# Token tiles of an output projection in the order 0, 3, 1, 2, 4, 5, with the norm of a tile at a higher scheduling priority

## The chip, the core and the metric

The kernel runs on one core of one Trainium2 chip. The metric is the device time of one execution in microseconds (us). The engines are TensorE (PE in the profile; PEld is its weight load), VectorE (DVE), ScalarE (ACT), GpSimd (POOL) and SyncE (SP), which only issues DMAs here. Each engine runs its own instructions strictly in order and waits on semaphores for the others.

## The reference

The kernel computes an encoder trunk of two layers for 768 tokens (256 and 512) with 1024 features. Each layer has a token mixer and then a gated feed-forward part, and both stand between two norms:

```python
def rms_norm(x, g):
    y = x * lax.rsqrt(jnp.mean(x * x, axis=-1, keepdims=True) + RMS_EPS)
    return y * g

def swiglu(h, w_gate_up, w_down):
    g, u = jnp.split(h @ w_gate_up, 2, axis=-1)
    return (jax.nn.silu(g) * u) @ w_down

for i in range(DEPTH):
    h = rms_norm(x, norm_mix_pre[i])
    m = window_gqa_sink(h, ...) if i % 2 == 0 else diff_attention(h, ...)   # both end in  o @ w_o
    x = x + rms_norm(m, norm_mix_post[i])
    h = rms_norm(x, norm_ffn_pre[i])
    x = x + rms_norm(swiglu(h, ffn_w_gate_up[i], ffn_w_down[i]), norm_ffn_post[i])
```

## The kernel before, in words

The 768 tokens are six tiles of 128 (`t` = 0 to 5). Every large product is made of three matmuls on split operands: a value is cut into a rounded part (`hi`, a cast on ACT) and the remainder (`lo`, a subtraction on DVE), and hi x hi, lo x hi and hi x lo are summed in PSUM (lines 266 to 268). `two_parts` does that for weights (lines 201 and 202), `split` for activations (lines 254 and 255). Weights come by DMA into two raw buffers (`wraw`), are split into a ring of five slots (`whi`, `wlo`), and a raw buffer's next DMA may go as soon as the split has read it.

`project` multiplies the mixer's output by `w_o` in two halves of 512 columns. The second half and everything behind it is `staged`: for each token tile it runs 24 matmuls (`po`), the square sum on ACT (line 506), and the four stages that `finish` returns. `stage_a` takes the row's reciprocal root (`rstd`: ACT line 310, POOL line 311), `stage_b` adds the normed product to the residual `x` (DVE line 421), stores `x` by SP and starts the next norm (`row_rstd`: ACT lines 316 and 310, POOL line 311), `stage_c` scales `x` into `y_po` (DVE line 320), and `stage_d` transposes that tile on PE and stores it as the feed-forward's input. The stages of a tile are written one and two rounds behind its matmuls.

The feed-forward's gate and up products use a seven-product scheme on 2 x 2 blocks. Tokens are halved into tiles 0 to 2 and 3 to 5, features into two blocks of 512, and `stage_d` is then `combine`. For tiles 0 to 2 it copies and splits the transposed tile (a11, a12). For tile t from 3 on it also needs tile t - 3 and makes the sums s1 to s4 (DVE lines 400, 401, 402 and 406) and splits them: five ACT casts and a copy, nine DVE operations. The same combination on the weights' side is lines 223 to 226, and `b` is the split of one weight block. The products follow in `ffn`: `p1` and `p2` (`px`, tiles 0 to 2, two groups of 12 matmuls for each of the first four chunks), then for each chunk `p4` (`pz`, needs the split of tile 5's second half), `p6` (`py`, needs s2), `p5` (`pw`, needs s1), `p7` (`py`, needs s3) and `p3` (`pw`, needs s4). The `px` groups need tiles 0 to 2 alone. All others need all of tiles 3 to 5 combined.

Code is written in program order, but a scheduler sets the order on each engine by priority and by its own estimate of when inputs are ready. Priority is the place in the program, unless a block is put under `tc.high_priority()`. The order that results is fixed when the program is built.

Of the kernel before, what the change touches and what calls it, by code (L numbers as in the profile page):

```python
# [13 lines left out]
ALU = mybir.AluOpType  # L14
# [15 lines left out]
NT = 6  # L30
# [14 lines left out]
def trunk(  # L45
# [19 lines left out]
    nc = tc.nc  # L65
# [22 lines left out]
    for name, step, mult in (("mask_l", 1, -1), ("mask_r", -1, 1)):  # L88
        m = const.tile([P, P], BF16, name=name)
        nc.gpsimd.memset(m, 0.0)  # L90
        nc.gpsimd.affine_select(
            out=m, in_=m, compare_op=ALU.is_ge, fill=MASK, base=0,
# [213 lines left out]
    def rstd(ss, eps, name):  # L306

        w = ss.shape[1]
        r = small.tile([P, 8], F32, tag="rstd", name=f"rstd_{name}")
        state["rstd"] = nc.scalar.activation(out=r[:, :w], in_=ss, func=AF.Identity, bias=eps)  # L310
        nc.gpsimd.tensor_tensor(out=r[:, :w], in0=r[:, :w], in1=mhalf[:, :w], op=ALU.pow)
        return r[:, :w]

    def row_rstd(src, junk, name):
        ss = small.tile([P, 1], F32, tag="ss", name=f"ss_{name}")
        nc.scalar.activation(out=junk, in_=src, func=AF.Square, scale=D ** -0.5, accum_out=ss)
        return rstd(ss, eps_sb[:, 0:1], name)

    def scaled(y, src, r, g):
        state["scaled"] = nc.vector.scalar_tensor_tensor(out=y, in0=src, scalar=r, in1=g, op0=ALU.mult, op1=ALU.mult)  # L320
# [24 lines left out]
    def load_x(sub, t):  # L345
        x = xpool.tile([P, D], F32, tag="x", name=f"x{sub}_{t}")
        nc.sync.dma_start(out=x, in_=x_at[sub][t])
        return x

    def transposes(src, t, name, scale=None):  # L350

        half, at = t // 3, (t % 3) * P

        def step(b):
            tp = bank(f"tp_{name}_{b}")
            for j in range(4):
                k = 4 * b + j
                nc.tensor.transpose(tp[:, j * P:(j + 1) * P], src[:, k * P:(k + 1) * P], ident)
            v = tp.rearrange("p (k n) -> p k n", k=4)
            h4 = h_hi[half][:, 4 * b:4 * b + 4, at:at + P]  # L360
            l4 = h_lo[half][:, 4 * b:4 * b + 4, at:at + P]
            if scale is None:
                split(h4, l4, v)
            else:
                nc.scalar.activation(out=h4, in_=v, func=AF.Copy, scale=scale)
                nc.vector.scalar_tensor_tensor(
                    out=l4, in0=v, scalar=scale, in1=h4.bitcast(F32), op0=ALU.mult, op1=ALU.subtract)

        return [lambda: step(0), lambda: step(1)]

    def combine(src, t, name, comb, o):

        at = (t % 3) * P

        def turn(b):  # L380
            tp = bank(f"tp_{name}_{b}")
            for j in range(4):
                k = 4 * b + j
                nc.tensor.transpose(tp[:, j * P:(j + 1) * P], src[:, k * P:(k + 1) * P], ident)
            return tp

        v4 = lambda v: v.rearrange("p (k n) -> p k n", k=4)
        into = lambda half, b: tuple(v[half][:, 4 * b:4 * b + 4, at:at + P] for v in (h_hi, h_lo))
        if t < 3:
            for b in range(2):  # L390
                tp = turn(b)
                split(*into(0, b), v4(tp))
                nc.scalar.copy(out=o[t][:, b * 512:(b + 1) * 512], in_=tp)
            return
        a11, a12 = o[t - 3][:, :512], o[t - 3][:, 512:]
        s1, a22, s3, s2 = o[t][:, :512], o[t][:, 512:], src[:, :512], src[:, 512:]
        tp1, tp0 = turn(1), turn(0)
        nc.scalar.copy(out=a22, in_=tp1)
        split(*into(1, 1), v4(tp1))
        nc.vector.tensor_tensor(out=s1, in0=tp0, in1=a22, op=ALU.add)  # L400
        nc.vector.tensor_tensor(out=s3, in0=tp0, in1=a11, op=ALU.subtract)
        nc.vector.tensor_tensor(out=s2, in0=s1, in1=a11, op=ALU.subtract)
        split(*(v[:, :, at:at + P] for v in comb["s2"]), v4(s2))
        split(*into(1, 0), v4(s3))
        split(*(v[:, :, at:at + P] for v in comb["s1"]), v4(s1))
        nc.vector.tensor_tensor(out=a12, in0=a12, in1=s2, op=ALU.subtract)
        split(*(v[:, :, at:at + P] for v in comb["s4"]), v4(a12))

    def finish(sub, t, o, ssy, x, g, comb):

        r = {}
        m, (ss, y) = o[t], ssy

        def stage_a():
            r[0] = rstd(ss[:, 1:2], ss[:, 0:1], f"post{sub}_{t}")

        def stage_b():  # L420
            nc.vector.scalar_tensor_tensor(out=x, in0=m, scalar=r[0], in1=x, op0=ALU.mult, op1=ALU.add)
            nc.sync.dma_start(out=x_at[sub + 1][t], in_=x)
            if g is not None:
                r[1] = row_rstd(x, y, f"pre{sub + 1}_{t}")

        def stage_c():
            scaled(y, x, r[1], g)

        def stage_d():
            if comb is not None:  # L430
                combine(y, t, f"h{sub + 1}_{t}", comb, o)
                return
            for s in transposes(y, t, f"h{sub + 1}_{t}"):
                s()

        return [stage_a, stage_b] + ([stage_c, stage_d] if g is not None else [])

    def last_tile(sub, t, m, ssy, x, r):

        halves = [slice(0, 512), slice(512, 1024)]  # L440
        for c, q in zip(halves, (nc.sync, nc.scalar)):
            nc.vector.scalar_tensor_tensor(
                out=x[:, c], in0=m[:, c], scalar=r, in1=x[:, c], op0=ALU.mult, op1=ALU.add)
            q.dma_start(out=x_at[sub + 1][t][:, c], in_=x[:, c])

    def staged(sub, units, o, sq, g, comb=None):

        st = {}
        for t in range(NT):
            x = load_x(sub, t)
            units[t][0]()
            if t >= 2 and g is not None:
                st[t - 2][2]()
            if t >= 1:
                st[t - 1][1]()
            units[t][1]()
            if t >= 2 and g is not None:  # L460
                st[t - 2][3]()
            if g is None and t == NT - 1:
                last_tile(sub, t, o[t], sq[t], x, sq["last"])
                break
            st[t] = finish(sub, t, o, sq[t], x, g, comb)
            st[t][0]()
        if g is None:
            return []
        return [st[NT - 2][2], st[NT - 1][1], st[NT - 2][3], st[NT - 1][2], st[NT - 1][3]]
# [214 lines left out]
    def project(o, layer, sub, turn_o, gp, g_next, wk, sq, done):  # L684
        gs = ExitStack()
        gpool2 = gs.enter_context(tc.tile_pool(name=f"comb{layer}", bufs=1, side="right", reuse_waits="tile"))
        comb = {
            n: tuple(gpool2.tile([P, 4, HALF], F32R, name=f"{n}{part}_{layer}") for part in ("hi", "lo"))
            for n in ("s1", "s2", "s4")}
        for t in range(done, NT):  # L690
            if turn_o is not None and t + 1 < NT:
                for s in turn_o(t + 1):
                    s()
            for s in out_unit(t, wk, o, 0, gp, sq, f"po{layer}_0_{t}"):
                s()
        wk = column_blocks(take(4), 512)
        units = {}
        for t in range(NT):
            steps = []

            def half(i, t=t, steps=steps):
                if i == 0:
                    steps += out_unit(t, wk, o, 1, gp, sq, f"po{layer}_1_{t}")
                n = len(steps) // 2
                for s in (steps[:n] if i == 0 else steps[n:]):
                    s()

            units[t] = [lambda half=half: half(0), lambda half=half: half(1)]
        return staged(sub, units, o, sq, g_next, comb), comb, gpool2, gs
# [177 lines left out]
    def ffn(layer, later, comb, cpool, cstack, ostack, gains):  # L887
# [116 lines left out]
        with ExitStack() as st:  # L1004
# [17 lines left out]
            for n2 in range(2):  # L1022
# [21 lines left out]
                else:  # L1044
# [25 lines left out]
                    if final:  # L1070
# [3 lines left out]

                        tails[NT - 1] = [last_first, lambda: piece(1)]
                    rest = staged(sub, tails, y, sq, g_next)
        return rest

# [81 lines left out]
    def rows(name):  # L1160
        stack = ExitStack()
        pool = stack.enter_context(tc.tile_pool(name=name, bufs=1, reuse_waits="tile"))
        return [pool.tile([P, D], F32, name=f"{name}{t}") for t in range(NT)], stack
# [5 lines left out]
    o, ostack = rows("oa")  # L1169
    later, *held = mixer_a(*gains(0), ready, o)  # L1170
    later = ffn(0, later, *held, ostack, lambda: gains(1))
    o, ostack = rows("ob")
# [69 lines left out]
```

## Time and profile before

| | us |
|---|---|
| median of 3 runs | 1755.25 |
| lowest and highest of them | 1753.36, 1756.82 |
| the profiled execution, its own time | 1756.35 |
| its span in the profile | 1754.6 |
| PE busy in the span | 1712.0 |
| DVE, ACT and POOL busy | 1174.0, 856.0, 81.6 |

PE is the engine to look at: it is busy in all but 43 us of the span. The kernel is long and most of it is a row of stages in which PE waits for nothing, so the stretches where it does wait must be looked for. "PEclk" or granted clock tells the share of full speed that TensorE had: 1.00 is 2.4 GHz and 0.50 is 1.2 GHz. A matmul that runs at 1.2 GHz counts as busy too, so time lost to the clock is not in PE's idle time.

Times "at 300" are microseconds from the start of the span. Layer 0's stretch around the change is at 265 to 345, layer 1's at 1190 to 1270.

### The profile page before, as it was taken

The page shows a single profiled execution, that of the slowest core. Times are in us where ns is not written, and L with a number is a line of the kernel's source. Part 1 is how long each engine was busy: PE and PEld are TensorE (multiplying, and loading weights), DVE is VectorE, ACT ScalarE, POOL GpSimd, SP SyncE. Part 2 cuts the span into 40 slices and gives each one's busy share as a digit, 9 for nine tenths or more (in the row PEclk, how much of TensorE's full clock was granted, in tenths as well). Part 3 has the DMA queues.
Part 4 walks back from the last instruction along what each step waited for, and adds up shares of the span by engine and source line. Part 5 has one row for each costly group of instructions (what it writes and reads, how often), then busy time and mean ns, then how long its engine had stood idle before and what let it go on. Part 6 is the DMA issues. An engine that isn't in the chain of part 4 may idle for free.

```text
span 1754.6 us, 25701 instructions
## 1 busy us (share of the span) xinstructions
PE 1712.0 (98%) x9714; PEld 1559.3 (89%) x9714; DVE 1174.0 (67%) x2368; ACT 856.0 (49%) x1971; POOL 81.6 (5%) x126
## 2 busy tenths in 40 slices
PE   8999999899999999999999999999799999999997
PEld 7888878799999988888999999878799999988886
DVE  7788767887777744446767677756887777744433
ACT  6777766433333333435566666756433333334432
POOL 1000001000000000002000000501000000000000
PEclk9999999899999999999999999999899999999999
DMA  6111105333332266454211111115333322266454
GB/s 205 37 37 46 47 15 191 121 131 100 100 101 72 94 202 190 150 163 173 85 37 37 37 42 42 48 37 182 119 132 100 100 100 75 87 201 195 142 156 138
DMA packets 55485, 187.14 MB, mean 107 GB/s; under 512 B 6721, under 2 KB 7105, under 8 KB 55361
## 3 DMA queue, kind: packets, MB, share of 16 engines
q1 hardware_dynamic: 51696, 167.93, 30.0%
q0 software_dynamic: 3520, 17.30, 2.5%
q8 instruction: 76, 1.25, 0.3%
q14 instruction: 49, 0.39, 0.1%
q10 hardware_dynamic: 144, 0.26, 0.0%
HBM read 155.59 MB, written 29.88 MB: 106 GB/s over the span
## 4 chain that ended last, share of the span: by engine, by line
PE 86%; DVE 6%; issue 3%; DMA 2%; ACT 2%; POOL 1%; SPq 0%; DVEq 0%; POOLq 0%; ACTq 0%
PE pd L266 6%; PE pd L268 6%; PE pd L267 6%; PE pqb L266 4%; PE pqb L268 4%; PE py L266 4%; PE pqb L267 4%; PE py L267 3%; PE py L268 3%; PE pw L266 3%; PE pw L267 3%; PE pw L268 3%; PE px L268 3%; PE px L267 3%; PE px L266 3%
## 5 line engine op out<-in xcount | busy, mean ns | idle before, releaser
L202 DVE TENSOR_TENSOR wlo<-wraw,whi 128x1024 fp32r<-128x1024 f32 (+1 forms) x206 | 239.3, 1166 | 122.1 <-ACT whi L201 120.8
L201 ACT CAST whi<-wraw 128x1024 fp32r<-128x1024 f32 (+1 forms) x206 | 204.9, 1001 | 169.6 <-PE px L267 84.2
L266 PE MATMUL pd<-whi,ahi 128*128 128x512 f32 (+1 forms) x550 | 210.4, 383 | 3.8 <-ACT ahi L254 3.8
L267 PE MATMUL pd<-wlo,ahi 128*128 128x512 f32 (+1 forms) x550 | 210.1, 382 | 0.0
L268 PE MATMUL pd<-whi,alo 128*128 128x512 f32 (+1 forms) x550 | 209.6, 382 | 0.0
L255 DVE TENSOR_TENSOR alo<-araw,ahi 128x768 fp32r<-128x768 f32 x88 | 84.1, 958 | 156.3 <-ACT ahi L254 154.7
L254 ACT CAST ahi<-araw 128x768 fp32r<-128x768 f32 x88 | 73.5, 835 | 171.3 <-PE pd L267 101.4
L266 PE MATMUL pqb<-whi,hhi 128*128 128x384 f32 x384 | 136.5, 356 | 0.0
L268 PE MATMUL pqb<-whi,hlo 128*128 128x384 f32 x384 | 128.8, 335 | 0.0
L267 PE MATMUL pqb<-wlo,hhi 128*128 128x384 f32 x384 | 128.8, 335 | 0.0
L266 PEld LDWEIGHTS pd<-whi,ahi 128*128 128x128 f32 x550 | 103.7, 189 | 24.6 <-ACT ahi L254 4.7
L268 PEld LDWEIGHTS pd<-whi,alo 128*128 128x128 f32 x550 | 103.9, 189 | 20.2
L267 PEld LDWEIGHTS pd<-wlo,ahi 128*128 128x128 f32 x550 | 103.7, 189 | 19.6
L266 PE MATMUL px<-hhi,whi 128*128 128x384 f32 x352 | 118.3, 336 | 2.2 <-ACT sv L912 2.2
L268 PE MATMUL px<-hhi,wlo 128*128 128x384 f32 x352 | 117.6, 334 | 0.0
L267 PE MATMUL px<-hlo,whi 128*128 128x384 f32 x352 | 117.6, 334 | 0.0
L942 ACT ACTIVATE u<-u 128x384 f32<-128x384 f32 x44 | 23.1, 525 | 161.2 <-DVE u L941 161.2
L266 PE MATMUL po<-whi,hhi 128*128 128x512 f32 x192 | 77.9, 406 | 0.2 <-ACT hhi L254 0.2
L268 PE MATMUL po<-whi,hlo 128*128 128x512 f32 x192 | 75.5, 393 | 0.2 <-DVE hlo L255 0.2
L267 PE MATMUL po<-wlo,hhi 128*128 128x512 f32 x192 | 75.3, 392 | 0.0
L266 PE MATMUL pqa<-whi,hhi 128*128 128x384 f32 x192 | 74.1, 386 | 0.1
L266 PEld LDWEIGHTS pqb<-whi,hhi 128*128 128x128 f32 x384 | 72.3, 188 | 1.9 <-issue 1.7
(244 smaller groups left out, 4422.8 us busy)
## 6 DMA issues: line engine op xcount, KB each, us to landing
araw<-act SPq DMA_DIRECT2D x88, 384.0 KB, 3.3
wraw<-in_wgu SPq DMA_DIRECT2D x62, 512.0 KB, 3.5
wraw<-in_wd SPq DMA_DIRECT2D x44, 512.0 KB, 4.2
y_wraw<-in_wgu SPq DMA_DIRECT2D x34, 512.0 KB, 3.5
act<-st POOLq DMA_DIRECT2D x44, 384.0 KB, 2.6
wraw<-in_wb SPq DMA_DIRECT2D x32, 384.0 KB, 3.1
xd<-x SPq DMA_DIRECT2D x18, 512.0 KB, 3.0
x<-xd SPq DMA_DIRECT2D x18, 512.0 KB, 4.2
```

The costliest lines, as they stand in the source:

```text
L201: state["raw_hi"] = nc.scalar.copy(out=hi, in_=src)
L202: state["raw_lo"] = nc.vector.tensor_tensor(out=lo, in0=src, in1=hi.bitcast(F32), op=ALU.subtract)
L254: state["hi"] = nc.scalar.copy(out=hi, in_=src)
L255: state["lo"] = nc.vector.tensor_tensor(out=lo, in0=src, in1=hi.bitcast(F32), op=ALU.subtract)
L266: nc.tensor.matmul(out, ah, bh, start=start and i == 0, stop=False, skip_group_check=more)
L267: nc.tensor.matmul(out, ah, bl, start=False, stop=False, skip_group_check=more)
L268: nc.tensor.matmul(out, al, bh, start=False, stop=stop and i == last, skip_group_check=more)
L942: nc.scalar.activation(out=u, in_=u, func=AF.Silu)
```

## The change

The second half of the output projection takes the tiles in the order 0, 3, 1, 2, 4, 5 in place of 0 to 5, so that tile 3 can be combined as soon as tile 0 has been. The norm's steps in `finish` (the reciprocal roots, the residual sum, the square sum and the scaling) get a higher priority. They apply to all four passes through `staged`; the new order only to the two that combine (`comb is not None`).

```diff
         def stage_a():
-            r[0] = rstd(ss[:, 1:2], ss[:, 0:1], f"post{sub}_{t}")
+            with tc.high_priority():
+                r[0] = rstd(ss[:, 1:2], ss[:, 0:1], f"post{sub}_{t}")
         def stage_b():
-            nc.vector.scalar_tensor_tensor(out=x, in0=m, scalar=r[0], in1=x, op0=ALU.mult, op1=ALU.add)
+            with tc.high_priority():
+                nc.vector.scalar_tensor_tensor(out=x, in0=m, scalar=r[0], in1=x, op0=ALU.mult, op1=ALU.add)
+                if g is not None:
+                    r[1] = row_rstd(x, y, f"pre{sub + 1}_{t}")
             nc.sync.dma_start(out=x_at[sub + 1][t], in_=x)
-            if g is not None:
-                r[1] = row_rstd(x, y, f"pre{sub + 1}_{t}")
         def stage_c():
-            scaled(y, x, r[1], g)
+            with tc.high_priority():
+                scaled(y, x, r[1], g)
...
-        st = {}
-        for t in range(NT):
+        st = []
+        for i, t in enumerate((0, 3, 1, 2, 4, 5) if comb is not None else range(NT)):
...
-            st[t] = finish(sub, t, o, sq[t], x, g, comb)
-            st[t][0]()
+            st.append(finish(sub, t, o, sq[t], x, g, comb))
+            st[i][0]()
```

The indices of `st` in the loop become `i - 2` and `i - 1` in place of `t - 2` and `t - 1`. No instruction is added or removed, and lines below the edit shift by 2 to 5.

The program that is built shows where instructions go. In the rows below, names end in a serial number, and the digit before it is the tile or the chunk (`y_po_1_5` is tile 5, `px_0` chunk 0). The first place is DVE in layer 0, around the scaling of the last tile (`y_po_1_5`). Before:

```order
L402 TENSOR_TENSOR y_po_1_4_4130<-oa_234,oa_231 128x512
L255 TENSOR_TENSOR s1lo_3844<-oa_234,s1hi_3843 128x4x128
L255 TENSOR_TENSOR hlo_114<-y_po_1_4_4130,hhi_112 128x4x128
L255 TENSOR_TENSOR s2lo_3846<-y_po_1_4_4130,s2hi_3845 128x4x128
L406 TENSOR_TENSOR oa_231<-oa_231,y_po_1_4_4130 128x512
L202 TENSOR_TENSOR wlo_4347<-wraw_4177,whi_4346 128x1024
L255 TENSOR_TENSOR s4lo_3848<-oa_231,s4hi_3847 128x4x128
L320 SCALAR_TENSOR_TENSOR y_po_1_5_4216<-x_5_4152,rstd_pre_5_4274,gpre_238 128x1024
L223 TENSOR_TENSOR wraw_4350<-wraw_4352,wraw_4350 128x512
L255 TENSOR_TENSOR hlo_114<-tp_h_5_1_4410,hhi_112 128x4x128
```

And now:

```order
L510 TENSOR_TENSOR oa_235<-po_1_5_4163,gpost_236 128x512
L255 TENSOR_TENSOR hlo_113<-tp_h_2_0_4228,hhi_111 128x4x128
L423 SCALAR_TENSOR_TENSOR x_5_4161<-oa_235,rstd_post_5_4244,x_5_4161 128x1024
L202 TENSOR_TENSOR wlo_4203<-wraw_4174,whi_4202 128x1024
L255 TENSOR_TENSOR hlo_113<-tp_h_2_1_4236,hhi_111 128x4x128
L255 TENSOR_TENSOR hlo_114<-tp_h_4_1_4307,hhi_112 128x4x128
L320 SCALAR_TENSOR_TENSOR y_po_1_5_4225<-x_5_4161,rstd_pre_5_4273,gpre_238 128x1024
L400 TENSOR_TENSOR oa_234<-tp_h_4_0_4312,oa_234 128x512
L401 TENSOR_TENSOR y_po_1_4_4139<-tp_h_4_0_4312,oa_231 128x512
L223 TENSOR_TENSOR wraw_4186<-wraw_4206,wraw_4186 128x512
```

Tile 5's scaling stood behind the whole combination of tile 4 and two weight splits; it now stands ahead of them, with tile 3's combination done earlier still and tile 2's split in its place. The second place is PE in layer 0, behind the last matmul of the projection. Before:

```order
L384 MATMUL tp_h_3_1_4219<-ident,y_po_1_3_4073 128x128 x4
L384 MATMUL tp_h_3_0_4224<-ident,y_po_1_3_4073 128x128 x4
L266 MATMUL px_0_4277<-hhi_111,whi_3898 128x384
L267 MATMUL px_0_4277<-hlo_113,whi_3898 128x384
L268 MATMUL px_0_4277<-hhi_111,wlo_3899 128x384
```

And now:

```order
L384 MATMUL tp_h_2_0_4228<-ident,y_po_1_2_4073 128x128 x4
L384 MATMUL tp_h_2_1_4236<-ident,y_po_1_2_4073 128x128 x4
L266 MATMUL px_0_4277<-hhi_111,whi_3898 128x384
L266 MATMUL px_1_4292<-hhi_111,whi_4170 128x384
L384 MATMUL tp_h_4_1_4307<-ident,y_po_1_4_4139 128x128 x4
L384 MATMUL tp_h_4_0_4312<-ident,y_po_1_4_4139 128x128 x4
L266 MATMUL px_2_4380<-hhi_111,whi_4182 128x384
L267 MATMUL px_0_4277<-hlo_113,whi_3898 128x384
```

The tile that is transposed directly ahead of `px` is now tile 2, which `px` itself needs, and tile 4's transposes moved ahead of nearly all of `px`. Tile 5's transposes stood behind all eight `px` groups and now stand behind six of them. Layer 1 has the same order, with other serial numbers.

## Rows read from the trace of the kernel before

**Rows 1.** Stretches of 50 us: length, PE, PEld, DVE, ACT, POOL busy (count), PEclk, DMA, GB/s

```profile
300.00:350.00 50.00, 41.69 (x208) 39.33 (x207) 42.15 (x63) 24.06 (x39) 1.94 (x3) 0.83 0.39 134
350.00:400.00 50.00, 50.00 (x288) 49.42 (x287) 41.50 (x62) 18.55 (x24) 2.17 (x4) 1.00 0.42 137
...
800.00:850.00 50.00, 48.93 (x280) 44.37 (x279) 37.76 (x68) 27.65 (x70) 9.15 (x12) 1.00 0.51 172
...
1200.00:1250.00 50.00, 43.92 (x237) 38.69 (x235) 38.72 (x50) 34.26 (x68) 5.65 (x10) 0.98 0.55 179
```

**Rows 2.** The same view in stretches of 5 us, layer 0

```profile
315.00:320.00 5.00, 2.16 (x12) 1.84 (x11) 5.00 (x8) 2.44 (x5) 0.00 (x0) 0.96 0.49 143
320.00:325.00 5.00, 2.67 (x10) 1.90 (x10) 2.11 (x4) 1.69 (x3) 0.00 (x0) 0.50 0.74 279
...
335.00:340.00 5.00, 5.00 (x26) 5.00 (x25) 2.63 (x4) 0.00 (x0) 0.00 (x0) 0.84 0.38 149
```

**Rows 3.** Waits of PE from 290 to 345: us in total, times, longest

```profile
PE tp_h L384 <- DVE y_po L320: 3.7, 1, 3.7
PE py L266 <- ACT s2hi L254: 2.1, 1, 2.1
PE pz L267 <- DVE hlo L255: 1.2, 1, 1.2
```

**Rows 4.** Timeline of PE, layer 0: start, length, instruction, idle before it and releaser

```profile
297.18 1.03 PE L384 MATMUL tp_h<-ident,y_po 128*128 128x128 f32 x8
297.97 0.42 PE L266 MATMUL px<-hhi,whi 128*128 128x384 f32 x1
...
320.86 1.94 PE L384 MATMUL tp_h<-ident,y_po 128*128 128x128 f32 x8 [3.70 <-DVE y_po L320]
...
342.09 0.33 PE L266 MATMUL pw<-s4hi,b 128*128 128x384 f32 x1
```

**Rows 5.** Timeline of PE, layer 1

```profile
1224.02 0.42 PE L266 MATMUL px<-hhi,whi 128*128 128x384 f32 x1
...
1268.11 0.34 PE L266 MATMUL pw<-s4hi,b 128*128 128x384 f32 x1
```

**Rows 6.** Timeline of DVE and POOL, layer 0: norms of tiles 3, 4 and 5

```profile
291.24 1.28 DVE L320 SCALAR_TENSOR_TENSOR y_po<-x,rstd_pre,gpre 128x1024 f32<-128x1024 f32 x1 [2.23 <-POOL rstd_pre L311]
298.82 1.28 DVE L320 SCALAR_TENSOR_TENSOR y_po<-x,rstd_pre,gpre 128x1024 f32<-128x1024 f32 x1 [0.84 <-POOL rstd_pre L311]
...
306.56 1.28 DVE L421 SCALAR_TENSOR_TENSOR x<-oa,rstd_post,x 128x1024 f32<-128x1024 f32 x1
310.94 0.69 POOL L311 TENSOR_TENSOR rstd_pre<-rstd_pre,mhalf 128x1 f32<-128x1 f32 x1 [10.42 <-ACT rstd_pre L310]
319.44 1.28 DVE L320 SCALAR_TENSOR_TENSOR y_po<-x,rstd_pre,gpre 128x1024 f32<-128x1024 f32 x1
```

**Rows 7.** Timeline of ACT, SP and DVE, layer 0: raw weights and their splits

```profile
301.07 1.05 ACT L201 CAST whi<-wraw 128x1024 fp32r<-128x1024 f32 x1 [1.18 <-DMA wraw<-in_wgu]
303.66 0.33 SPq L196 DMA_DIRECT2D wraw<-in_wgu  x1
308.13 0.69 DVE L223 TENSOR_TENSOR wraw<-wraw,wraw 128x512 f32<-128x512 f32 x1 [0.29 <-DMA wraw<-in_wgu]
308.74 0.68 DVE L255 TENSOR_TENSOR hlo<-tp_h,hhi 128x512 fp32r<-128x512 f32 x1
318.95 0.33 SPq L196 DMA_DIRECT2D wraw<-in_wgu  x1
323.61 0.69 DVE L223 TENSOR_TENSOR wraw<-wraw,wraw 128x512 f32<-128x512 f32 x1 [2.89 <-DMA wraw<-in_wgu]
332.57 1.22 DVE L202 TENSOR_TENSOR wlo<-wraw,whi 128x1024 fp32r<-128x1024 f32 x1
```

**Rows 8.** Stretches of 5 us elsewhere, each with one wait of PE

```profile
645.00:650.00 5.00, 3.89 (x11) 3.12 (x12) 3.05 (x3) 1.90 (x3) 0.00 (x0) 0.72 0.85 248
...
1570.00:1575.00 5.00, 3.09 (x14) 2.21 (x13) 2.96 (x3) 2.62 (x3) 0.00 (x0) 1.00 0.77 226
```

More of the change, by code (lines that the diff above doesn't have):

```diff
@@ L446, in staged @@
     def staged(sub, units, o, sq, g, comb=None):
-        st = {}
-        for t in range(NT):
+        st = []
+        for i, t in enumerate((0, 3, 1, 2, 4, 5) if comb is not None else range(NT)):
             x = load_x(sub, t)
             units[t][0]()
[L455 to L458, printed above, removed]
+            if i >= 2 and g is not None:
+                st[i - 2][2]()
+            if i >= 1:
+                st[i - 1][1]()
             units[t][1]()
-            if t >= 2 and g is not None:
-                st[t - 2][3]()
+            if i >= 2 and g is not None:
+                st[i - 2][3]()
             if g is None and t == NT - 1:
```

## The prediction

> **What bounds the kernel now.** I read the table of 50 us stretches first. From 350 to 400 PE has no idle time, the full clock, and 288 matmuls in 50 us, which is 0.174 us each and 2.08 us for a group of 12 [rows 1]. That is the common state, and a change off PE's path is worth nothing there. From 300 to 350 PE lacks 8.3 us and the granted clock is 0.83, and from 1200 to 1250 it lacks 6.1 us [rows 1]. Both lie where the mixer's output projection passes into the feed-forward, and there the change is made.
>
> The 5 us stretches narrow it down. The clock is lost from the end of 315 to 320 (0.96, so the last 0.4 us are at half), is 0.50 from 320 to 335 (one such row stands for three), and costs 1.6 us more from 335 (0.84). That is 17.0 us at 1.2 GHz, which begin when PE has been busy for only 2.16 us of 5 [rows 2]. The waits say for what PE stood still: 3.7 us for `y_po`, tile 5's scaled norm, and then 1.2 and 2.1 us for the splits of tile 5's combination [rows 3].
>
> The loss as a whole is a difference of dates. From the first `px` matmul at 297.97 to the first `pw` matmul on s4 at 342.09 [rows 4] PE does thirteen groups of 12 (eight `px`, two `py`, one `pw`, two `pz`) and two rounds of transposes. A round takes 0.79 us (297.18 to 297.97) [rows 4]. So 13 x 2.08 + 2 x 0.79 = 28.6 us of work took 44.1 us: 15.5 us are lost. Layer 1 takes 1224.02 to 1268.11, also 44.1 us [rows 5], and loses the same. These 31 us are all that the edit can win there.
>
> Why `y_po` of tile 5 was late is in DVE's and POOL's rows. Its residual sum starts at 306.56, its reciprocal root is taken at 310.94 and ends at 311.63, but the scaling starts at 319.44 [rows 6]: 7.8 us in which DVE did the combination of tile 4 and weight splits that stand ahead of it in its order. The residual sum had itself waited behind tile 3's combination.
>
> **Part 1, the reordered norms: what goes away.** Tile 3 is combined two rounds earlier, and tile 5's norm is no longer behind a combination. I walk the new order with the durations of before. Neighbouring DVE operations of 512 columns start 0.60 apart (308.13, 308.74) [rows 7], and the 1024-column ones I take at 1.15 to 1.2. The three rounds of transposes and six tiles of matmuls ahead of `px` are as many as before, so PE reaches 297.97 at the same time. DVE takes tile 3's sums (nine operations, 5.4 us, less two splits that moved behind) where it stood idle for 2.23 us each round [rows 6]. Tile 4's scaling, which ran 298.82 to 300.1 [rows 6], I put at 300.3; if none of the idle time could be used it would end 2 us later. Behind it on DVE are a weight split, a product of tile 5 with the gain, and half of tile 2's split (1.15 + 0.6 + 0.6, to 302.7), then tile 5's residual sum at 303.9, against 307.8 before. ACT's square sum and the root on ACT and POOL stand behind one weight cast and a copy, and I get `y_po` of tile 5 at 308.2, where before it was 320.7. PE wants it behind six `px` groups, at 314.7: the 3.7 us wait goes, with 6 us to spare.
>
> **Part 2, what it adds on PE.** `px` needs tiles 0 to 2, and tile 2 is now transposed directly ahead of it. Its first matmul waits for an ACT cast (1.6 us), tile 4's transposes for `y_po` of tile 4 (0.4 us), and the second `px` matmul for tile 2's split at 302.7. By then PE has done one round of transposes and three matmuls (1.3 us), so this new wait costs 302.7 - 297.97 - 1.3 = 3.4 us; the ends are 1.6, if the split were on time, and 5.4, with the 2 us above. From 302.7 the rest of six `px` groups (69 matmuls, 12.0 us) reaches 314.7, transposes 315.5, two more groups 319.7.
>
> **Part 3, what is late next.** The weights of the first full chunk are prepared from a raw tile whose DMA waits for a buffer. That buffer's split needs an ACT cast (301.07 before) [rows 7] that now stands behind tile 4's copy and cast; I get its split at 305.2, against 303.6. From issue to use the DMA took 303.66 to 308.13, 4.47 us [rows 7], so the data come at 309.7. On DVE behind them are eight operations of 0.60, then 1.15 + 1.2 + 1.15, to 318.0, then 1.2 for the split that `pz` needs: 319.2. PE is there at 319.7, no wait. The next raw tile's DMA can go at 318.0 (318.95 before) and takes 4.66 us (318.95 to 323.61) [rows 7], so 322.6. Four DVE operations later, at 325.0, is s2's remainder. PE, after `pz` and 12 matmuls of `py` and `pw` at 323.9, waits 1.1 us, runs 12 more to 327.1, waits 0.9 us for the second chunk's last weight split (325.0 + three sums, 1.15, 0.6, 1.15 = 329.7, with nine matmuls ahead of it), and has the remaining 22 done at 333.5. Seven of these belong to a later group in the old order (1.2 us): the same work is done at 332.3 instead of 342.1, **9.8 us less**.
>
> From this I take off 0.5 us for the next chunks, whose `py` matmuls moved ahead of `pz`, so that weights have less cover, and 0.8 us for some half-clock time in the new waits. That is **8.5 us a layer, 17.0 for both**.
>
> **Part 4, queues and the other passes.** On SP a raw tile for chunk 2 moves ahead of two that are wanted sooner; it waits only for tile 2's transposes, which are done at 298, before its neighbours can go. A gain load moves ahead of the next weights and waits for tile 5's norm, 308.2, when the buffer behind it is not free before 315. Both cost nothing as long as the norm is early; if it were as late as before (320.7), the weights would be 2 us late. Between the feed-forward of layer 0 and mixer 1 the priority alone acts. PE lacks 1.07 us from 800 to 850 [rows 1], so between 1.1 gained and about as much lost by splits that now stand behind a 1.2 us norm; I take 0.3 gained. The last pass keeps its order.
>
> **The sum.** 17.0 + 0.3 = 17.3 us. The span goes from 1754.6 to 1737.3, the profiled execution's 1756.35 to 1739.05; it lies 1.1 above the median of the runs, so the median goes from 1755.25 to **1738.0**.
>
> **Rivals.** (a) *The second chunk's weights keep their dates.* In before their last split ran from 332.57, to 333.8 [rows 7], with PE not yet there. If DVE, which has as many operations as ever, is no earlier, `pz` of chunk 1 waits until then: 333.8 + 3.8 - 1.2 = 336.4, 5.7 us a layer, 1755.25 - 11.4 = 1743.9. For it: DVE was busy for all of 315 to 320 [rows 2]. Against it: DVE stood idle for 2.89 us on the raw data [rows 7], and sums of tile 5 now fit in there.
>
> (b) *The clock.* The new wait at `px` leaves PE idle for 3.2 of 4.7 us, about as sparse as the stretch ahead of 320. Elsewhere a shorter idle time was followed by half clock once (0.72, with 1.1 us idle in the stretch) and not at all another time (1.00, with 1.9 us idle) [rows 8]. If `px` gets one low stretch as long as before, 17.0 us, half of it is lost: PE is at 328.2 instead of 319.7. The weights are then no limit, the remaining 67 matmuls (11.7 us) end at 339.9, less 1.2 is 338.7: 3.4 us a layer, 1748.4. The Trainium skill (TensorE: Matmul & The Clock Gate, section "HAM oscillation — how this bites in real kernels") describes groups of matmuls that each begin at the low clock because each has first waited for its data. By that rule the change would only move the cold start from tile 5's products to `px`; the rows agree in one of the two stretches.
>
> (c) *Slower.* The same mechanism, if the low clock holds for all of `px` and its transposes: 17.0 us of work at half speed ends at 336.7, the rest at 348.4, less 1.2 is 347.2, against 342.1. That loses 5.1 us a layer, 1765.5. It decides from a low stretch of 2 x (342.1 - 330.2) = 24 us on; the longest in the rows is 17.0.
>
> (d) *It doesn't do what it says.* The order on DVE and PE is known, so only an input that comes late could undo it, such as the DMA that feeds `pz`. With it two waits would trade places: 1755.
>
> (e) *Better.* The waits at 323.9 and 327.1 (2.0 us) don't come, and the clock stays up: about 11 us a layer and 1 more, 1732.
>
> **How the numbers follow.** Forecast 0.60 (own range 1734 to 1743), (a) 0.18, (b) 0.10, (c) 0.04, (d) 0.04, (e) 0.04. The range from 1732 to 1747 leaves out (b), (c) and (d). A measurement of this kernel tells about 0.2%, 3.5 us, from no change: faster 0.92, same 0.04, slower 0.04.
>
> **What would show it.** Right: no wait of PE for `y_po` of tile 5 in either layer; that scaling at 305 to 311; a new wait of 1.6 to 5.4 us ahead of the second `px` matmul; the stretch from the first `px` to the first `pw` on s4 down from 44.1 to about 35 us. Wrong: `pz` waiting for weights behind 320 (rival a), or a granted clock of 0.50 through `px` (b, c).

## The result, and the profile after

| | before | after |
|---|---|---|
| median | 1755.27 us (4 runs) | 1740.85 us (4 runs, 1740.23 to 1745.47) |
| ratio after / before, 95% interval | | 0.9924 (0.9904 to 0.9944) |
| profiled execution, own time | 1756.35 us | 1740.31 us |
| its span | 1754.6 us | 1738.5 us |

The changed kernel is 14.4 us faster, 2.9 us short of the forecast's gain, and inside the range. The two profiled executions are 16.0 us apart, because the one before lies 1.1 us above its median and the one after 0.5 us below. The waits of PE in layer 0, from 290 to 345 (engine, line, what it waited for: us in total, times, longest), which answer [rows 3]:

```profile
PE py L267 <- DVE s2lo L255: 2.0, 1, 2.0
PE px L266 <- ACT hhi L254: 1.4, 1, 1.4
PE px L267 <- DVE hlo L255: 1.1, 1, 1.1
PE pz L266 <- ACT whi L201: 0.6, 2, 0.4
PE tp_h L384 <- DVE y_po L320: 0.3, 1, 0.3
```

The 3.7 us wait for tile 5's scaled norm is gone (the 0.3 that is left is tile 4's). New are 2.5 us at `px`, and `py` now waits for s2's remainder. PE's timeline of the changed kernel, layer 0 (start, length, instruction, idle before it and releaser), which answers [rows 4]:

```profile
296.61 1.03 PE L384 MATMUL tp_h<-ident,y_po 128*128 128x128 f32 x8
299.01 0.62 PE L266 MATMUL px<-hhi,whi 128*128 128x384 f32 x2 [1.37 <-ACT hhi L254]
299.93 1.09 PE L384 MATMUL tp_h<-ident,y_po 128*128 128x128 f32 x8 [0.30 <-DVE y_po L320]
302.26 0.44 PE L267 MATMUL px<-hlo,whi 128*128 128x384 f32 x1 [1.06 <-DVE hlo L255]
314.35 1.03 PE L384 MATMUL tp_h<-ident,y_po 128*128 128x128 f32 x8
319.39 0.33 PE L266 MATMUL pz<-hhi,whi 128*128 128x384 f32 x1
325.72 0.44 PE L267 MATMUL py<-s2lo,whi 128*128 128x384 f32 x1 [2.01 <-DVE s2lo L255]
328.88 0.69 PE L266 MATMUL pz<-hhi,whi 128*128 128x384 f32 x1 [0.19 <-ACT whi L201]
336.34 0.45 PE L266 MATMUL pw<-s4hi,b 128*128 128x384 f32 x1
```

Tile 5's transposes (314.35) wait for nothing. The first `pw` on s4 starts at 336.34, and twelve `py` matmuls (2.08 us) that stood behind it before now stand ahead of it, so the same work is done at 334.26, where it was 342.09. Layer 1, the same view, which answers [rows 5]:

```profile
1252.67 0.44 PE L266 MATMUL pw<-s4hi,b 128*128 128x384 f32 x1 [0.85 <-DVE st L937]
```

DVE and SP in layer 0, which answer [rows 6, 7]: tile 5's scaling, the issue of the next raw tile, its first use, s2's remainder, and the second chunk's last weight split.

```profile
305.83 1.28 DVE L320 SCALAR_TENSOR_TENSOR y_po<-x,rstd_pre,gpre 128x1024 f32<-128x1024 f32 x1
317.30 0.33 SPq L196 DMA_DIRECT2D wraw<-in_wgu  x1
323.14 0.69 DVE L223 TENSOR_TENSOR wraw<-wraw,wraw 128x512 f32<-128x512 f32 x1 [1.66 <-DMA wraw<-in_wgu]
324.99 0.68 DVE L255 TENSOR_TENSOR s2lo<-y_po,s2hi 128x512 fp32r<-128x512 f32 x1
329.14 1.22 DVE L202 TENSOR_TENSOR wlo<-wraw,whi 128x1024 fp32r<-128x1024 f32 x1
```

And the stretches (length, PE, PEld, DVE, ACT, POOL busy, granted clock, DMA, GB/s), which answer [rows 1, 2, 8]:

```profile
325.00:330.00 5.00, 4.08 (x15) 3.58 (x16) 5.00 (x8) 2.52 (x3) 0.00 (x0) 0.73 0.32 106
330.00:335.00 5.00, 5.00 (x28) 5.00 (x28) 2.46 (x5) 0.00 (x0) 0.00 (x0) 0.93 0.63 209
...
640.00:645.00 5.00, 5.00 (x24) 4.11 (x23) 1.25 (x2) 0.22 (x1) 0.00 (x0) 1.00 0.79 276
...
800.00:850.00 50.00, 50.00 (x301) 46.55 (x300) 41.47 (x87) 30.86 (x80) 5.59 (x9) 1.00 0.49 167
...
1555.00:1560.00 5.00, 4.24 (x12) 3.37 (x13) 2.96 (x3) 1.54 (x2) 0.00 (x0) 0.66 0.79 260
```

In layer 0 the clock was at half speed for 17.0 us before [rows 2]. Now it is for 5 x (0.27 + 0.07) / 0.5 = 3.4 us, behind the 2.0 us wait of `py`. From 800 to 850 PE has no idle time.

**Where the time came from.** The same instructions in both traces, as dates. Before:

```profile
635.84 0.39 PE L266 MATMUL pd<-whi,ahi 128*128 128x512 f32 x1
...
1158.53 0.62 PE L775 MATMUL bsc<-kb,qb 128*128 128x512 f32 x2
...
1562.23 0.39 PE L266 MATMUL pd<-whi,ahi 128*128 128x512 f32 x1
1745.11 0.28 PE L268 MATMUL pd<-whi,alo 128*128 128x256 f32 x1
```

After:

```profile
628.77 0.39 PE L266 MATMUL pd<-whi,ahi 128*128 128x512 f32 x1
...
1148.84 0.63 PE L778 MATMUL bsc<-kb,qb 128*128 128x512 f32 x2
1545.48 0.39 PE L266 MATMUL pd<-whi,ahi 128*128 128x512 f32 x1
1729.94 0.28 PE L268 MATMUL pd<-whi,alo 128*128 128x256 f32 x1
```

| stretch | lead at its end | gained in it |
|---|---|---|
| start to the transposes ahead of `px`, layer 0 | 0.57 | 0.57 |
| to the first down product (`pd`), layer 0 | 7.07 | 6.50 |
| to mixer 1's last scores (`bsc`) | 9.69 | 2.62 |
| to the first down product, layer 1 | 16.75 | 7.06 |
| to the last down product | 15.17 | -1.58 |
| to the end of the span | 16.1 | 0.9 |

The two stretches around the edit gave 13.6 us. Not all of it is waiting that went: PE's 9714 matmuls were busy for 1712.0 us before and for 1704.5 us after, so some 7.5 of the 16.1 us are time that as many matmuls no longer lost to the clock, and 8.6 us are idle time. The -1.58 is not the edit's: PE waits 1.9 us at the first `pd` in either kernel and layer, and half clock followed in layer 0 before (0.72) and not in layer 1 (1.00) [rows 8], and after the change the other way round (1.00 from 640 to 645, 0.66 from 1555 to 1560). The same 1.58 stands with a plus in the 2.62, so that 1.0 is left for the transition between the layers. The 0.6 at the start and the 0.9 at the end lie where the edit moves nothing that PE waits for; the tail behind the last matmul took 8.6 us in this execution and 9.3 in another of the same kernel (after_again, below).

### The profile page after: what moved, and what is told of

Read it like the earlier page. It is cut to its first block, busy times and chain, and to the rows that moved or that the text cites. A ratio compares the mean times of both kernels' runs of the same rounds, so it can differ in the third digit from the quotient of the medians.

```text
span 1738.5 us, 25699 instructions
## 1 busy us (share of the span) xinstructions
PE 1704.5 (98%) x9714; PEld 1552.1 (89%) x9714; DVE 1172.6 (67%) x2368; ACT 854.7 (49%) x1971; POOL 82.3 (5%) x126
```

## The experiments

Each kernel ran against the kernel before on the same chip. The table gives all, with their intervals.

| kernel | median us | ratio to before (95%) |
|---|---|---|
| order_only | 1752.7 | 0.9988 (0.9978 to 0.9998) |
| prio_only / prio_only_again | 1740.7 / 1742.0 | 0.9925 (0.9910 to 0.9940) / 0.9922 (0.9908 to 0.9935) |
| after_again (the changed kernel) | 1742.1 | 0.9926 (0.9913 to 0.9938) |
| s2_first | 1742.8 | 0.9930 (0.9916 to 0.9945) |
| w_s2_first | 1741.1 | 0.9921 (0.9903 to 0.9940) |
| t2_first | 1740.0 | 0.9905 (0.9890 to 0.9921) |
| s4b_pool | 1754.1 | 0.9990 (0.9981 to 0.9999) |
| less_dve | 1734.7 | 0.9884 (0.9872 to 0.9897) |
| up1_y | 1742.7 | 0.9930 (0.9917 to 0.9942) |
| up1_y_t2 | 1744.2 | 0.9940 (0.9928 to 0.9952) |
| up1_y_prio | 1743.3 | 0.9935 (0.9923 to 0.9947) |

**Which half of the edit.** First each half alone. order_only takes the priority out, here and in `stage_b` and `stage_c`:

```diff
-            with tc.high_priority():
+            if True:
                 r[0] = rstd(ss[:, 1:2], ss[:, 0:1], f"post{sub}_{t}")
...
```

> The new tile order without the priority: tile 5's scaling stands behind the whole combination of tile 4 and both weight splits again. My theory: the gain needs both halves of the edit, because DVE must get tile 3's sums out of the way and also take tile 5's norm before tile 4's sums. Then the scaling of tile 5 starts at about 319 in layer 0 (319.44 before, 305.83 with the whole edit), PE waits some 2 us for it behind px, the s2 remainder of tile 5 comes at 328 to 329, the low clock comes back, and the time is 1751 us (1747 to 1756). Rival: the early combination of tile 3 is what pays and the norm comes early by itself; then there is no wait for y_po of tile 5 in layer 0 and the time is about 1742 us.

Tile 5's scaling on DVE and PE's wait for it, order_only, layer 0:

```profile
318.08 1.27 DVE L320 SCALAR_TENSOR_TENSOR y_po<-x,rstd_pre,gpre 128x1024 f32<-128x1024 f32 x1
...
319.50 1.06 PE L384 MATMUL tp_h<-ident,y_po 128*128 128x128 f32 x8 [1.02 <-DVE y_po L320]
```

As expected, the scaling is nearly as late as before (319.44 [rows 6]) and the gain is 2 us. PE's wait for it was 1.0 us, not 2, and the low clock hardly came back (3.4 us of it in layer 0, 17.0 before); but this execution took 1748.3 us, 4.3 below the median of its kernel. prio_only keeps the tiles in the order 0 to 5:

```diff
-        for i, t in enumerate((0, 3, 1, 2, 4, 5) if comb is not None else range(NT)):
+        for i, t in enumerate(range(NT)):
```

> The priority with the tiles in the order 0 to 5. My theory: tile 5's scaling moves to 306 to 308 in layer 0 and the 3.7 us wait for it goes, but DVE must then do the sums of both tile 3 and tile 4 behind it (10 us), so tile 5's own split comes at about 322 and pz waits for it for 4 to 6 us, with half clock behind it; the time is 1748 us (1744 to 1753). Together with the order alone the two halves then give less than the whole edit's 14.4 us. Rival: the priority does all of it and the order nothing; then the time is about 1741 us, and there is no wait over 2 us at pz.

PE and DVE of prio_only, layer 0 (`pz` of the first chunk, its second matmul, `pz` of the second chunk, and that chunk's last weight split):

```profile
315.99 0.34 PE L266 MATMUL pz<-hhi,whi 128*128 128x384 f32 x1
320.25 0.69 PE L267 MATMUL pz<-hlo,whi 128*128 128x384 f32 x1 [3.92 <-DVE hlo L255]
329.39 0.44 PE L266 MATMUL pz<-hhi,whi 128*128 128x384 f32 x1 [0.40 <-ACT whi L201]
329.65 1.22 DVE L202 TENSOR_TENSOR wlo<-wraw,whi 128x1024 fp32r<-128x1024 f32 x1
```

The wait came as I expected, 3.9 us at `pz` for tile 5's split, and the time did not: 1740.7 (this execution took 1745.1). My theory that both halves are needed has fallen, because I had left out what the tile order costs: the `px` wait of 3.5 us in the changed kernel is missing here, and PE comes to `pz` at 315.99 instead of 319.39. Both kernels start `pz` of the second chunk at nearly the same date, 329.39 and 328.88. The two then ran once more, side by side.

> The changed kernel itself, on one chip with the next three. The first runs gave the same time for the priority alone (1740.7) as for the whole edit (1740.9), so my theory that both halves are needed has fallen. New theory: DVE's work up to the second chunk's weights sets the end of the stretch, and in both kernels pz of that chunk starts at 329 (328.88 and 329.39 in layer 0); the tile order only moves a wait from pz to px. Expected: 1741 us, within 2 us of the priority alone. Rival: the order is worth something that the noise of the first runs hid; then this kernel is 2 to 5 us faster than the priority alone.

> The priority with the tiles in the order 0 to 5, for the comparison with the run before it. Theory: 1741 us, within 2 us of the changed kernel. Rival: 1743 to 1746.

1742.1 and 1742.0: whatever the tile order gives or takes on top of the priority is less than the some 3 us that the two intervals can hide. **Within these 3 us the priority alone gives the whole gain.**

**Is it one late instruction?** s2_first puts s2's split at the higher priority (its edit is shown), w_s2_first the first full chunk's weight sums and splits as well:

```diff
-        split(*(v[:, :, at:at + P] for v in comb["s2"]), v4(s2))
+        with tc.high_priority():
+            split(*(v[:, :, at:at + P] for v in comb["s2"]), v4(s2))
```

> The changed kernel, with the split of s2 at a higher priority too, so that tile 5's remainder of s2 is ahead of the weight sums which wait for the raw tile's DMA (it would be done at 322 instead of 325.6 in layer 0). My theory: the new 2.0 us wait of py (1.3 in layer 1) is only the first place where PE meets the raw tile that lands at 323; without it PE runs 12 matmuls on and waits for the second chunk's weight cast, which depends on the same DMA and comes at most 0.6 us earlier. So the py wait goes, a wait of 1.5 to 2.5 us for whi stands at pz, and the time is 0.6 us a layer better, with up to 1.7 more if the dip in the clock goes: 1739.5 us (1737.5 to 1741). Rival: the wait is DVE's order alone; then 2.0 + 1.3 + 1.7 = 5 us go and the time is 1736.

> As the run before it, and the first full chunk's weight sums and splits are put at a higher priority as well, so the raw buffer that they read comes free about 1.2 us earlier. My theory, that the DMA of the next raw tile sets the end of this stretch: its issue moves from 317.3 to about 316 in layer 0, the second chunk's weights come 1.2 + 0.6 us earlier, and the time is 1.8 us a layer better than the changed kernel, 1737 us (1735 to 1739.5). Rival: the weights are not what ends last; then this kernel has the time of the run before it within 0.5 us.

`pz` of the first and of the second chunk in s2_first, then the raw tile's first use, `py` and `pz` of the second chunk in w_s2_first:

```profile
321.34 0.33 PE L266 MATMUL pz<-hhi,whi 128*128 128x384 f32 x1
329.04 0.44 PE L266 MATMUL pz<-hhi,whi 128*128 128x384 f32 x1 [1.30 <-ACT whi L201]
```

```profile
322.06 0.69 DVE L226 TENSOR_TENSOR wraw<-wraw,wraw 128x512 f32<-128x512 f32 x1 [1.54 <-DMA wraw<-in_wgu]
...
323.22 0.44 PE L271 MATMUL py<-s2hi,whi 128*128 128x384 f32 x1 [1.56 <-ACT s2hi L259]
328.97 0.45 PE L271 MATMUL pz<-hhi,whi 128*128 128x384 f32 x1 [0.87 <-ACT whi L203]
```

s2_first did what I expected to the waits: the 2.0 us at `py` went, and PE met the weights at `pz` instead. Its time is no better (1742.8, outside my 1737.5 to 1741). The trace shows one thing more: `px` ran partly at half clock here (6.8 us of it, from 300 to 310), so PE came to the first `pz` at 321.34, 5.4 us later than in prio_only (315.99), and to the second at the same date as there, within 0.4 us. A date at which PE arrives is not what sets the end. In w_s2_first the raw tile came 1.1 us earlier, and `pz` started at 328.97 all the same: here my expectation of 1.8 us a layer was wrong. t2_first takes away part of the `px` wait (PE's timeline stands behind the expectation):

```diff
-                split(*into(0, b), v4(tp))
+                with tc.high_priority():
+                    split(*into(0, b), v4(tp))
```

> The changed kernel with tile 2's split at the higher priority too. The new wait at px, 3.5 us in layer 0 (302.26 less 297.4 less 1.3 of work), should fall to about 1.5 to 2, since the first remainder of tile 2 is ready at about 300 in place of 302.1. Theory that DVE's work and the second chunk's weights bound the stretch: PE only comes to pz of that chunk earlier and waits there, which starts at 329 as before, and the time stays at 1741 us within 1.5. Rival: the px wait is paid at the end in full; then 2 us a layer go and the time is 1737.

```profile
299.85 0.44 PE L267 MATMUL px<-hlo,whi 128*128 128x384 f32 x1 [1.29 <-DVE hlo L255]
...
330.08 0.69 PE L266 MATMUL pz<-hhi,whi 128*128 128x384 f32 x1 [3.87 <-ACT whi L201]
```

PE was 2.4 us earlier at the second matmul of the first `px` group (299.85), and stood 3.9 us at `pz` of the second chunk, which started no earlier. (This execution took 1744.9.) The median is 2 us below the changed kernel's on the same chip; the two intervals (0.9890 to 0.9921, 0.9913 to 0.9938) still overlap, so a small gain is neither shown nor excluded.

**Is it DVE's amount of work?** In five orders of the same instructions that have the priority, `pz` of the second chunk starts between 328.9 and 330.1; the changed kernel alone has 328.88 in one execution and 330.04 in another (after_again). What they share is the list of DVE operations up to there. This date does not give the time by itself: order_only has 328.04 and is 10 us slower, because PE had done less by then. Two kernels change the list. s4b_pool moves eight operations of each layer to POOL (`first_chunk` holds the first two full chunks):

```diff
-        nc.vector.tensor_tensor(out=a12, in0=a12, in1=s2, op=ALU.subtract)
-        split(*(v[:, :, at:at + P] for v in comb["s4"]), v4(a12))
+        nc.gpsimd.tensor_tensor(out=a12, in0=a12, in1=s2, op=ALU.subtract)
+        split(*(v[:, :, at:at + P] for v in comb["s4"]), v4(a12), nc.gpsimd)
...
-                two_parts(*b22s[i], b22)
+                two_parts(*b22s[i], b22, nc.gpsimd if i in first_chunk else None)
```

> The changed kernel with work taken off DVE: the subtraction for s4, its remainder, and the remainder of the plain weight block b of the first two full chunks run on POOL, which is nearly idle there. That is 8 of DVE's operations of 0.60 us in the stretch, 2.4 us of them ahead of the next raw tile's DMA and 1.8 behind it. Theory that DVE bounds the stretch through the second chunk's weights: that raw tile's DMA goes 1.2 to 2.4 us earlier, those weights are split at about 326 in place of 329.1, pz of the second chunk starts 2 to 3 us earlier, and the time is 1736 us (1734 to 1739). Rival: the DMA or ACT bounds it, or a busy POOL slows DVE's operations down; then the time is 1741 or more, and DVE's 128x512 operations last longer than 0.60.

POOL, DVE and PE of s4b_pool, layer 0:

```profile
308.65 0.55 POOL L313 TENSOR_TENSOR rstd_pre<-rstd_pre,mhalf 128x1 f32<-128x1 f32 x1 [5.95 <-ACT rstd_pre L312]
...
312.30 0.69 DVE L404 TENSOR_TENSOR y_po<-oa,oa 128x512 f32<-128x512 f32 x1
312.39 1.73 POOL L204 TENSOR_TENSOR b<-wraw,b 128x512 fp32r<-128x512 f32 x1 [3.20 <-DVE wraw L225]
312.90 1.78 DVE L226 TENSOR_TENSOR wraw<-wraw 128x512 f32<-128x512 f32 x1
...
333.72 0.44 PE L268 MATMUL pz<-hhi,whi 128*128 128x384 f32 x1 [1.95 <-ACT whi L203]
```

The last case of the rival came true: a DVE operation beside one of POOL's takes 1.78 us in place of 0.69. There are eight such pairs up to 333, with 0.9 to 1.1 us each, so DVE lost some 8.4 us and saved 8 x 0.60 = 4.8. `pz` of the second chunk is 4.8 us later than in the changed kernel (333.72), and the kernel 12 us slower. (The norm's roots stand in POOL's queue too, but the queue did not hold them up: POOL stood idle ahead of tile 5's root, the first row, and waited for ACT.) So this run does not test DVE's work taken away, but DVE's work made longer. less_dve leaves the eight operations out, with none of them on POOL:

```diff
-        nc.vector.tensor_tensor(out=a12, in0=a12, in1=s2, op=ALU.subtract)
-        split(*(v[:, :, at:at + P] for v in comb["s4"]), v4(a12))
+        nc.scalar.copy(out=comb["s4"][0][:, :, at:at + P], in_=v4(a12))
...
-                two_parts(*b22s[i], b22)
+                if i in first_chunk:
+                    nc.scalar.copy(out=b22s[i][0], in_=b22)
+                    b22s[i] = b22s[i][0], b22s[i][0]
...
```

> The changed kernel with part of the computation left out: the subtraction for s4 and its remainder, and the remainder of the plain weight block b of the first two full chunks of each layer. The rounded part stands in for the remainder, so PE's matmuls stay as many; only DVE loses eight operations of 0.60 us in the stretch, and POOL is not used, which in the run before made DVE's neighbouring operations 1.1 us longer. Theory that DVE bounds the stretch through the second chunk's weights: in layer 0 the raw tile's DMA is issued at 315 to 316 (317.30 in the changed kernel), the last split of these weights ends 2.5 to 3.5 us earlier than 330.3, pz of the chunk starts at 326 to 327 in place of 328.88, and the time is 1736 us (1734 to 1738.5). Rival: ACT's casts or the DMA bound it; then pz starts at 328 to 329 and the time stays at 1741 us.

```profile
326.43 0.44 PE L272 MATMUL pz<-hhi,whi 128*128 128x384 f32 x1 [0.58 <-ACT whi L203]
```

`pz` of the second chunk at 326.43 and 1734.7 us, as the theory had it: 4.8 us less of DVE's work a layer, 2.5 us earlier at `pz`, 7.4 us off the whole. More work for DVE and less of it move the time both ways. The 2.5 us are not simply doubled, though. In layer 0 only 1.2 us of them are left at the first down product (627.62, in the changed kernel 628.77), since PE then waited 1.3 us at `py` for another operation of DVE and lost 1.7 us to half clock; layer 1 gave 4.0 us, without half clock.

**Or the DMA?** up1_y loads the up weights of that chunk into a buffer that is free some 19 us earlier:

```diff
-            raw_src.append((wgu[layer, c, 1], 1024, "y" if 1 < c < NCH - 3 else "w"))
+            raw_src.append((wgu[layer, c, 1], 1024, "y" if 0 < c < NCH - 3 else "w"))
```

> The changed kernel with the second full chunk's up weights loaded into one of the y buffers, whose DMA can go at 298.6 in layer 0, instead of a raw buffer that comes free at 317.30. Only the gate weights then wait for a raw buffer (issued at 314.96 in the changed kernel). Theory that DVE's order and this DMA bound the stretch together: DVE's idle time ahead of the sums (1.66 us in layer 0) goes, the second chunk's weights are split by 329 in place of 330.3, but tile 5's split now stands behind a sum that waits for the gate weights until 319.5 to 320.5, which costs pz of the first chunk 0.5 to 1.5 us; the time is 1739.5 us (1737 to 1741.5). Rival: the DMA's date doesn't matter, since DVE has the same number of operations; then 1741 to 1742 us.

```profile
318.94 0.68 DVE L223 TENSOR_TENSOR wraw<-y_wraw,wraw 128x512 f32<-128x512 f32 x1
...
325.71 0.45 PE L266 MATMUL py<-s2hi,whi 128*128 128x384 f32 x1 [2.46 <-ACT s2hi L254]
```

DVE's wait for the raw tile is gone (its sum runs at 318.94 in place of 323.14) and `pz` waits for no weights. Now s2 is late, 2.5 us in layer 0, since DVE made the weights first. The time is nearest to the rival's, 1742.7. So the DMA's date is worth nothing by itself that the intervals show. (In this execution, too, `px` ran partly at half clock, so PE came to the first `pz` at 321.00; it then waited for s2 all the same.) Two more kernels joined this edit with t2_first's and with prio_only's.

> The run before with tile 2's split at the higher priority, which alone gave 1740.0 against 1742.1 us for the changed kernel on the same chip. Theory: with the DMA off the path some of the px wait that this removes (2.5 us a layer to 1.7) reaches the end; 1738 us (1735.5 to 1740.5). Rival: it is given back at pz as before, and the time is that of the run before it within 1 us.

> The up weights in a y buffer with the priority alone, the tiles in the order 0 to 5. Theory: as with the tile order, the time is within 2 us of that kernel (1739.5 us): no px wait, but 4 us at pz for tile 5's split. Rival: without the DMA wait the tile order begins to matter, since the early combination of tile 3 is then what lets the weights come early; then this kernel is 2 to 4 us slower than it.

1744.2 and 1743.3 us. Neither is better (for the first I had expected 1738), and with the DMA off the path the tile order still makes no difference that shows. Of the kernels that leave nothing out, none is faster than the changed one beyond the intervals.

## Why the prediction was right, and where it was not

**What bounds the kernel**: right. Both stretches gave what the edit won, and stretches without idle time gave nothing. A large part of the sum rests on the clock: the forecast counted the whole 15.5 us a layer as lost, half clock included, and let the full clock hold but for 0.8 us. That came true within 0.9 us in both layers of this execution.

**Part 1**: right. Tile 5's scaling ran from 305.83 to 307.1, forecast done by 308.2, and PE's transposes at 314.35 did not wait for it.

**Part 2**: right in place and size. The second matmul of the first `px` group started at 302.26 (forecast 302.7). From the end of the transposes (296.61 + 0.79 = 297.40) less 1.3 us of work that is a cost of some 3.5 us, forecast 3.4.

**Part 3** is where the sum is too high. PE reached `pz` at 319.39 without a wait (forecast 319.7), and the raw tile's DMA was issued at 317.30 (318.0). But from issue to use it took 5.84 us, not the 4.66 of before [rows 7], so s2's remainder ended at 325.7 instead of 325.0 and the wait was 2.0 us instead of 1.1. The clock cost 3.4 / 2 = 1.7 us in layer 0 instead of 0.8. Relative to the transposes the same work was done 342.09 - 334.26 - 0.57 = 7.3 us earlier, where 9.8 less 0.8 for the clock was forecast, so 1.7 us are missing. Counted from the end of the transposes, s2's remainder let PE go on 1.3 us later than forecast (28.3 us behind them instead of 27.0) and the clock cost 0.9 us more; some 0.5 us came back behind that, mostly because the wait for the second chunk's weights was 0.6 us, not 0.9. In layer 1 it was 1268.11 - (1252.67 - 2.08) - 9.69 = 7.8 us without any loss of clock; there `pw` waited 0.85 us for an operation on DVE (the row at 1252.67), for which the sum had no term. The later chunks took 0.8 in each layer, not 0.5. In all 6.5 and 7.1 us a layer in place of 8.5.

**Part 4**: the transition gave 1.0, the upper end of its bounds, not 0.3.

**Rivals.** (a) did not come as stated: the second chunk's last weight split ended at 330.4, not at 333.8, and the forecast's 329.7 was nearer. `pz` did wait for these weights, 0.6 us in layer 0, where the forecast had 0.9. But (a) names what the experiments point to as the bound of the changed kernel, DVE with as many operations as ever: waits that are taken away at `px` or `py` come back at `pz`, and only less work on DVE gave time beyond the intervals. The forecast walked PE's and DVE's dates and so had the waits at `px`, `py` and `pz` nearly right for this one order. What it did not see is that they can be exchanged: rival (e) counts the waits at 323.9 and 327.1 as time to be won, while s2_first took the first away and won nothing. (b) half clock in `px`: not in this execution, though in layer 1 of another of the same kernel (below), for 6.8 us and not 17. Its row with 1.1 us idle had cut a wait in two: PE waits 1.9 us at the first `pd` in both layers, so a shorter wait is not what its two rows show. Its 3.2 us idle at `px` is 3.4 by the forecast's own dates. (c), (d) and (e) did not come.

**What the prediction did not ask** is which half of the edit pays. The new order was forecast to pay, since tile 3's sums would run where DVE stood idle. They do, but in DVE's busy time the priority alone does nearly as much. The stretch from 265 to 325, before, order_only, prio_only and after:

```profile
265.00:325.00 60.00, 53.79 (x277) 46.82 (x275) 45.41 (x57) 39.17 (x79) 6.75 (x12) 0.95 0.54 187
```

```profile
265.00:325.00 60.00, 54.52 (x280) 47.70 (x279) 47.23 (x60) 39.72 (x81) 7.61 (x12) 0.98 0.53 184
```

```profile
265.00:325.00 60.00, 56.08 (x288) 50.20 (x287) 48.64 (x63) 40.54 (x82) 7.05 (x12) 0.95 0.52 185
```

```profile
265.00:325.00 60.00, 55.98 (x296) 49.36 (x294) 48.97 (x64) 40.67 (x82) 7.59 (x12) 1.00 0.54 184
```

DVE (the third busy time) got through 45.4 us of work before, 48.6 with the priority and 49.0 with both. The 3.6 us more match the 3.4 us by which the second chunk's last split moved (332.57 [rows 7] to 329.14). My reading, which no run isolates, is that a norm that comes early lets PE transpose early, and so feeds DVE; the sums of tile 3 are only another thing to feed it with. And PE, which no longer stands still for tile 5's norm, kept its clock where it had lost it, which is nearly half of the gain between the two profiled executions (7.5 of 16.1 us).

## What to carry to other kernels

When one engine prepares everything that another consumes, several waits at different instructions can be one bound: add up the preparing engine's work to the last date that matters before a gain is booked for each wait. Test it by changing the amount of that work and not only its order. An operation on the longest chain (here a norm through three engines) should go ahead of bulk work on a shared in-order queue, and here that alone gave the whole gain within the noise. Try the halves of an edit apart: the half that looks like the idea may be the one that gives nothing.

## What the runs showed of the hardware

**DVE beside POOL.** A 128x512 operation on POOL (1.3 to 1.7 us) made the DVE operation beside it some 1.1 us longer, 0.69 to 1.78, as the rows of s4b_pool show. POOL ran from 312.39 to 314.12, and the DVE operation that began at 312.90 ended at 314.68, 0.56 us behind it. The Trainium skill (SBUF — State Buffer, section "SBUF: two separate sides") says that a DVE operation with two inputs in SBUF and a POOL operation that reads SBUF lock a shared pair of ports: the one that starts first has it for its whole instruction, and the other is blocked. These rows agree.

**The clock is a matter of the execution.** In layer 1 the changed kernel had full clock through `px` in the first profile (`px` starts at 1215.8 there, and no stretch of it is below 1.00), and in another execution (after_again), with waits at `px` that were no longer (1.3 and 0.8 us instead of 1.4 and 1.1), this:

```profile
1220.00:1225.00 5.00, 4.19 (x18) 3.79 (x17) 5.00 (x7) 3.75 (x6) 0.00 (x0) 0.55 0.96 372
1225.00:1230.00 5.00, 5.00 (x24) 5.00 (x24) 3.21 (x5) 2.51 (x6) 0.55 (x1) 0.77 0.68 216
```

That is 5 x (0.45 + 0.23) / 0.5 = 6.8 us at half clock, in an execution of 1745.6 us; the first took 1740.3. The drop behind the first `pd` cost 1.58 us in the table above, and after_again has it in both layers (0.66 from 640 to 645, 0.68 from 1560 to 1565). With the 3.4 us in `px` it lost some 5.1 us more to the clock than the first execution, about the 5.3 us by which the two differ. Not every such loss counts in full: PE came later to `py`, and its wait there was 0.3 us instead of 1.3. Executions of the changed kernel differ by 4 to 5 us, and a trace of one execution should be read together with its own time.
